# Layer 1's projection as Strassen products of column-tile pairs, with queries and gates kept in DRAM

## The chip, the cores and the metric

One core of one Trainium2 chip runs the whole program. The metric is device microseconds of one execution. Three runs of the kernel before gave 1135.93, 1138.13 and 1138.16 us; the median is 1138.13 us. One further execution was profiled: it took 1137.09 us, of which the trace covers a span of 1135.4 us. TensorE (PE) does the matrix products, VectorE (DVE) and ScalarE (ACT) the element-wise work, GpSimd (POOL) some of it, and SyncE (SP) mostly issues DMAs.

## The reference

A two-layer decoder trunk over 1024 positions of width 1024. Layer 0 is a pooling and short-convolution mixer; layer 1 is sliding-window attention with 16 query heads, 2 key/value heads and a gate. Only layer 1 is changed:

```
y = rms_norm(h, norm_g[1])
proj = y @ w_in + b_in                       # 1024 -> 1024 q | 128 k | 128 v | 1024 z
q = partial_rotary(q.reshape(b, s, 16, 64), cos, sin)     # first 16 dims of each head turn
k = partial_rotary(k.reshape(b, s, 2, 64), cos, sin)
attn = sliding_window_gqa_sinks(q, k, v, sinks)           # 8 blocks of 128 queries, window 128
h = h + (attn * jax.nn.silu(z)) @ w_out + b_out
return rms_norm(h, final_norm_g)
```

## The kernel before

All products are float32-accurate: each operand is split into a high part that TensorE multiplies in its fast float32 mode and a low part that holds the rest (`split`, L179 the cast on ACT, L180 the subtraction on DVE), and three matmuls (high by high, high by low, low by high) stand for one.

**Layer 0's input projection** (to 532 us of the span) is feature-major: the weights are the stationary operand, 512 tokens move. It goes by pairs of column tiles. For each pair, seven products of 4 x 3 matmuls do what eight would do plainly (Strassen's scheme in Winograd's form): three sums of weight quarters before (L409 to L413), seven splits, and five sums of results after (L463 to L477). The products are at L440. Twelve of them are done ahead, with results stored in `c_dram`, while the other operands are still being made.

**Layer 0's output projection** (532 to 718 us, L800 to L802) gives h transposed; each tile gets its residual, is scaled by the norm's gain and split, and is put aside in `h_dram` in another layout (L754, L755).

**Layer 1's projections** are plain: keys and values (`kv`, L186 to L188, 718 to 743 us) and queries (743 to 833 us) are token-major, with h as the stationary operand; each result takes the row's RMS factor and the bias on DVE (L880, L909) and the rotary turn on POOL (L860 to L865). Gates (`gate1`, L1008 to L1018, 833 to about 938 us) are feature-major; DVE multiplies by the RMS row, ACT applies Silu. Queries stay in SBUF as `qt`, gates as `sz`. Block 0's scores run between the gates.

**The attention loop** takes blocks of 128 queries. In its turn `b` it makes the queries' transposed split form for block `b + 1` (`queries`: cast L935, subtraction on POOL L936, transposes on PE L939, copy L941), turns block `b`'s probabilities (`probs`: PE transposes L1058, POOL selects L1064 and L1067), computes scores of `b + 1` (L960, L961; masks and maxima on DVE L963 to L969; Exp on ACT L972), projects block `b - 1` (L1113 to L1115), and attends block `b` (L1081, gate at L1092, split into `aH` and `aL`). `finish` normalises and stores the output (L1129, L1130, L1150). The turn b = 1 begins at 940.2 us, the turn b = 7 at 1098.4, and the last one, which only projects, at 1116.8.

The order on each engine comes from a scheduler that follows dependences; on each engine instructions run strictly in that order, so an instruction that waits holds those behind it. SP issues all DMAs of the kernel before.

Of the kernel before, what the change touches and what calls it, by code (L numbers as in the profile page):

```python
# [78 lines left out]
def trunk(ctx, tc, x, xT, g1, pos, cols, w_in, w_pool, w_out, w_q, w_kv, w_z, b_q, b_kv,  # L79
               sinks, w_o, g_fin, out):  # L80
# [201 lines left out]
    def load_to(n):  # L282
        while len(raws) < min(n, len(units)):
            src, shape, _, _ = units[len(raws)]
            raws.append(W(shape))
            nc.sync.dma_start(out=raws[-1], in_=src)

    def split_to(n):
        load_to(n)
        while len(done) < min(n, len(units)):  # L290
            i = len(done)
            _, shape, alloc, parts = units[i]
            n_ = shape[1] // parts
            res = []
            for j in range(parts):
                h, lo = alloc(F32R), alloc(F32R)
                split(h, lo, raws[i][:, j * n_:(j + 1) * n_])
                res += [(h[:, k, :], lo[:, k, :]) for k in range(n_)]
            done.append(res)
# [945 lines left out]
```

## Time and profile before

| | us |
|---|---|
| median of three runs | 1138.13 |
| profiled execution, whole | 1137.09 |
| its span | 1135.4 |
| PE busy in the span | 1078.5 |
| DVE busy | 783.5 |
| ACT busy | 463.5 |
| POOL busy | 224.6 |

"Busy" counts the time in which an engine has an instruction under way. Matmuls are pipelined, so that one 512-column matmul is listed with about 0.4 us, though another starts every 0.23 us; a stretch where PE is busy all the time is read by the starts. The share over the span hides that stages have different limits, so the rows below are by stage. In rows of groups the columns are: line, engine, operation, output<-input, shapes, count | busy us in all, mean ns of one | idle us of the engine just before, and who ended it.

### The profile page before, as it was taken

Reading aid. Unit: us, or ns where it says so; the run is one execution under the profiler, and the core shown is the slowest. Engines: PE = TensorE matmul, PEld = TensorE weight load, DVE = VectorE, ACT = ScalarE, POOL = GpSimd, SP = SyncE. Lnnn points to the kernel's source line nnn. Section 1 sums busy time; section 2 is a strip of 40 time slices with the busy share of each in tenths; the row PEclk is TensorE's granted clock in tenths of the full one; section 3 lists DMA queues with packets and bytes.
Section 4 is the critical chain, followed back from the end, with each engine's and each line's share of the span. In section 5 each row is a group of like instructions: output and inputs, shape, how many; then the busy total and the mean of one; then the engine's idle time right before and its main releaser. Section 6 shows DMA issues by size and latency. Waiting matters only on the chain.

```text
span 1135.4 us, 14172 instructions
## 1 busy us (share of the span) xinstructions
PE 1078.5 (95%) x5020; PEld 873.1 (77%) x5020; DVE 783.5 (69%) x1392; ACT 463.5 (41%) x961; POOL 224.6 (20%) x396
## 2 busy tenths in 40 slices
PE   4989999999999999999999999999999997898897
PEld 3767788888888888887788788988888885676776
DVE  4699879967696669866645854721143679889995
ACT  4753332423233332334324423320023777777653
POOL 0000000000000000000001010333320226788874
PEclk9999999999999999999999999999999999999999
DMA  5342331221212212126653334410022305370001
GB/s 204 112 167 99 141 128 38 93 84 38 93 38 96 81 56 75 65 75 226 222 203 134 137 142 146 165 38 19 1 93 96 127 24 125 57 93 20 20 20 56
DMA packets 70694, 109.09 MB, mean 96 GB/s; under 512 B 37472, under 2 KB 37600, under 8 KB 70624
## 3 DMA queue, kind: packets, MB, share of 16 engines
q1 hardware_dynamic: 70624, 108.20, 28.9%
q8 instruction: 39, 0.64, 0.2%
q14 instruction: 31, 0.25, 0.1%
HBM read 89.04 MB, written 19.14 MB: 95 GB/s over the span
## 4 chain that ended last, share of the span: by engine, by line
PE 79%; DVE 12%; ACT 5%; issue 2%; DMA 2%; POOL 0%; SPq 0%; DVEq 0%; ACTq 0%
PE b L440 38%; PE psD L801 3%; PE psD L802 3%; PE psA L800 2%; PE psD L800 2%; PE psA L802 2%; PE psA L801 2%; PE psA L186 2%; PE psD L186 2%; PE psA L187 2%; PE psA L188 2%; PE psD L188 2%; PE psD L187 2%; ACT pt L972 1%; DMA W<-w_in 1%
## 5 line engine op out<-in xcount | busy, mean ns | idle before, releaser
L179 ACT CAST W<-W 128x512 fp32r<-128x512 f32 (+1 forms) x199 | 143.9, 731 | 357.9 <-DVE W L180 108.5
L180 DVE TENSOR_TENSOR W<-W 128x512 fp32r<-128x512 f32 (+1 forms) x199 | 162.6, 823 | 115.2 <-ACT W L179 68.6
L690 POOL MEMSET T<- 128x16 f32 x8 | 0.9, 111 | 358.4 <-DVE T L624 229.2
L818 POOL TENSOR_TENSOR t<-t,T 128x512 f32<-128x512 f32 x14 | 19.4, 1387 | 248.5 <-ACT T L817 248.5
L440 PE MATMUL b<-B11h,W 128*128 128x512 f32 x192 | 65.6, 405 | 2.7 <-ACT W L179 1.8
L440 PE MATMUL b<-T2h,W 128*128 128x512 f32 x192 | 64.5, 396 | 2.2 <-ACT W L179 2.2
L440 PE MATMUL b<-B22h,W 128*128 128x512 f32 x192 | 64.7, 398 | 1.2 <-DVE T L469 1.1
L440 PE MATMUL b<-T1h,W 128*128 128x512 f32 x192 | 64.4, 396 | 0.0
L440 PE MATMUL b<-T3h,W 128*128 128x512 f32 x192 | 64.3, 396 | 0.0
L440 PE MATMUL b<-B21h,W 128*128 128x512 f32 x192 | 63.9, 396 | 0.0
L440 PE MATMUL b<-T4h,W 128*128 128x512 f32 x192 | 63.5, 391 | 0.0
L972 ACT ACTIVATE pt<-psB,smax 128x128 f32<-128x128 f32 x128 | 45.4, 366 | 24.8 <-DVE smax L969 19.6
L801 PE MATMUL psD<-U,W 128*128 128x512 f32 x128 | 51.5, 402 | 2.6 <-DVE U L180 2.6
L802 PE MATMUL psA<-U,W 128*128 128x512 f32 x128 | 50.4, 394 | 1.4 <-DVE W L180 1.4
L960 PE MATMUL psB<-kT,qT 128*128 128x256 f32 (+1 forms) x128 | 34.8, 294 | 17.3 <-ACT qT L941 7.6
L802 PE MATMUL psD<-U,W 128*128 128x512 f32 x128 | 50.9, 398 | 0.2 <-DVE W L180 0.2
L800 PE MATMUL psD<-U,W 128*128 128x512 f32 x128 | 51.1, 399 | 0.0
L800 PE MATMUL psA<-U,W 128*128 128x512 f32 x128 | 50.8, 397 | 0.0
L1113 PE MATMUL psD<-O,aH 128*128 128x512 f32 (+1 forms) x128 | 50.7, 396 | 0.0
L801 PE MATMUL psA<-U,W 128*128 128x512 f32 x128 | 50.6, 395 | 0.0
L1115 PE MATMUL psD<-O,aL 128*128 128x512 f32 (+1 forms) x128 | 49.7, 388 | 0.0
L1114 PE MATMUL psD<-O,aH 128*128 128x512 f32 (+1 forms) x128 | 49.6, 387 | 0.0
(330 smaller groups left out, 2923.6 us busy)
## 6 DMA issues: line engine op xcount, KB each, us to landing
W<-w_in SPq DMA_DIRECT2D x54, 512.0 KB, 3.5
W<-w_out SPq DMA_DIRECT2D x32, 512.0 KB, 3.8
W<-w_z SPq DMA_DIRECT2D x16, 512.0 KB, 3.5
O<-o_dram SPq DMA_DIRECT2D x31, 256.0 KB, 5.5
o_dram<-t SPq DMA_DIRECT2D x30, 256.0 KB, 2.0
T<-xT SPq DMA_DIRECT2D x16, 256.0 KB, 4.3
h_dram<-T SPq DMA_DIRECT2D x16, 256.0 KB, 2.1
W<-w_q SPq DMA_DIRECT2D x8, 512.0 KB, 4.4
```

Of the source, the lines that this page charges most:

```text
L179: nc.scalar.copy(out=dst_h, in_=src)
L180: sub(out=dst_l, in0=src, in1=dst_h.bitcast(F32), op=ALU.subtract)
L186: mm(dst, lhsT=ah, rhs=bh, start=(i == 0), stop=False)
L187: mm(dst, lhsT=ah, rhs=bl, start=False, stop=False)
L440: mm(dst, lhsT=w[:, hw, k], rhs=x[hx][:, k], start=start and k + n == 0, stop=k == 3 and n == 2, skip_group_check=not start)
L800: mm(dst, lhsT=w[k][0], rhs=oHL[f][0], start=(f == 0), stop=False)
L801: mm(dst, lhsT=w[k][0], rhs=oHL[f][1], start=False, stop=False)
L802: mm(dst, lhsT=w[k][1], rhs=oHL[f][0], start=False, stop=(f == 15))
L972: exps.append(act(out=res[g][:, 2 * i2 + i, :], in_=bv[:, i, P:256], func=AF.Exp, scale=0.125, bias=smax[:, at + i:at + i + 1], accum_out= ...
L1113: mm(o, lhsT=a[0][:, kk, :], rhs=woH[8 * n + k][:, c], start=(k == 0), stop=False)
L1114: mm(o, lhsT=a[0][:, kk, :], rhs=woL[8 * n + k][:, c], start=False, stop=False)
L1115: mm(o, lhsT=a[1][:, kk, :], rhs=woH[8 * n + k][:, c], start=False, stop=(k == KT - 1))
```

## The change

The class `Strassen` now holds the seven-product scheme, used for layer 0 as before and for layer 1's whole projection (`st1`): nine pairs of column tiles, first the pair (k, v), then four pairs of query tiles, then four of gate tiles. The query columns are reordered so that the first two tiles hold the 16 turning dimensions of all heads.

- `operands` and the norm: h scaled by the gain stays in SBUF as `Y`; the RMS factor is multiplied into it (`normed1`) and the quarters' sums and splits are made (B11, B21, then T1 to T4, B22), partly during layer 0's output projection, partly during 18 products done ahead (`AHEAD1 = 9`), whose results go to `c1_dram` and come back. The RMS sums move from POOL to DVE.
- `kv`: the pair's tiles are transposed on PE to token-major per block. The cos and sin tables are transposed to feature-major.
- `q_pair`, `turn_pair`, `q_store`: bias and turn in feature-major form on DVE, split into high and low, stored to `q_dram`: high from ACT's queue, low from SP's. `load_q` reads them per half block, on POOL's queue; there are no query transposes.
- `z_pair`, `gates`: Silu on ACT, stored to `z_dram` from ACT's queue, read back by SP per half block in `attend`, where one multiplication takes the place of two.
- Scores of blocks 0 and 1, and block 0's probabilities and attention, run between the gate pairs' products; the loop starts at b = 1. Of the eight output weight pieces, four are fetched at the end of the pairs and split as b = 1 begins (`WO_FIRST`), the rest in b = 1 (`WO_PLAN`), all subtractions on DVE.

```
-def queries(b, js): ... for g in range(2):
-            nc.scalar.copy(out=qs[:, :, 0, :], in_=q)
-            ptt(out=qs[:, :, 1, :], in0=q, in1=qs[:, :, 0, :].bitcast(F32), op=ALU.subtract)
-                tr(bank[:, i * P:(i + 1) * P], qs[:, i].rearrange("p a d -> p (a d)"), identr)
-            nc.scalar.copy(out=t, in_=bank.bitcast(F32))
+    def load_q(b, js):
+            for g, t in enumerate(qTs[b, js]):
+                h = 8 * g + 4 * js
+                nc.gpsimd.dma_start(out=t.rearrange("p (h c) -> p h c", c=P), in_=q_dram[
+                    :, :, h:h + 4, b * P:(b + 1) * P].rearrange("a d h c -> (a d) h c"))
+    def queries(b, js):
+        load_q(b, js)
+        load_q(*((b, 1) if js == 0 else (b + 1, 0)))
...
+    st1 = Strassen(w_l1, [(8, 9)] + [(2 * i, 2 * i + 1) for i in (0, 1, 2, 3, 5, 6, 7, 8)],
+                   AHEAD1, c1_dram, ...)
+    st1.store = nc.scalar.dma_start
+    def q_store(t, s, x, biased):
+        hi, lo = t3(F32R), t3()
+        ...
+            act(out=hi, in_=x, func=AF.Identity, bias=col(C_BQ, t))
+            stt(out=lo, in0=x, scalar=col(C_BQ, t), in1=hi.bitcast(F32), op0=ALU.add,
+                op1=ALU.subtract)
+        for j, o in enumerate((hi.bitcast(F32), lo)):
+            (nc.sync if j else nc.scalar).dma_start(out=q_dram[j, 8 * t:8 * t + 8, :, hs(s)]...)
+    def gates():
+        for at_, s_, c in z_out:
+            act(out=c, in_=c, func=AF.Silu, bias=col(C_BZ, at_))
+        for at_, s_, c in z_out:
+            nc.scalar.dma_start(out=z_dram[at_, :, hs(s_)], in_=c)
...
-            tt(out=at[:, 2 * jj:2 * jj + 2, :], in0=at[:, 2 * jj:2 * jj + 2, :],
-               in1=sz[4 * s + 2 * js + jj][:, :, bb * P:(bb + 1) * P], op=ALU.mult)
+        nc.sync.dma_start(out=zt, in_=z_dram[4 * js:4 * js + 4, :, b * P:(b + 1) * P].rearrange(
+            "m p c -> p m c"))
+        tt(out=at, in0=at, in1=zt, op=ALU.mult)
...
-        nc.sync.dma_start(out=out[b * P:(b + 1) * P, :], in_=h2)
+        nc.scalar.dma_start(out=out[b * P:(b + 1) * P, :], in_=h2)
+    for n, k2 in WO_FIRST:
+        load_wo(n, k2)
+    for b in range(1, NB + 1):
```

Three places show how the order moves. ACT's order before, where block 0's Exp (L972) first stands between the gates' Silu (L1018); a table load stands at each change from one function to the other:

```order
L1018 ACTIVATE U<-U,colt 128x512
L179 CAST W<-W 128x1024
L972 ACT_TABLE_LOAD
L972 ACTIVATE pt_7001,den<-psB,smax 128x128 x4
L179 CAST O_7249<-W 128x512
L179 CAST O_7253<-W 128x512
L972 ACTIVATE pt_7002,den<-psB,smax 128x128 x2
L941 CAST qT<-psB 128x512 x2
L972 ACTIVATE pt_7002,den<-psB,smax 128x128 x2
L979 ACTIVATE es<-es 128x8
L1018 ACT_TABLE_LOAD
L1018 ACTIVATE U<-U,colt 128x512
```

ACT's order now, at the same place among the gate pairs (L1117 is Silu, L1092 Exp, L1119 the gates' store):

```order
L1092 ACT_TABLE_LOAD
L1092 ACTIVATE pt_6964,den<-psB,smax 128x128 x2
L180 CAST W<-W 128x512
L1092 ACTIVATE pt_6972,den<-psB,smax 128x128 x2
L180 CAST W<-S_7023 128x512
L1117 ACT_TABLE_LOAD
L1117 ACTIVATE t_6979<-t_6979,colt 128x512
L1092 ACT_TABLE_LOAD
L1092 ACTIVATE pt_6964,den<-psB,smax 128x128 x2
L1092 ACTIVATE pt_6972,den<-psB,smax 128x128 x2
L1092 ACTIVATE pt_6965,den<-psB,smax 128x128 x2
```

The functions change more often: 15 table loads stand from the first of these to block 2's Exp, 7 before from the first shown to the end of the program.

POOL's order before, in one half block of the attention loop (L983 scales the probabilities, L936 is the queries' low part, L1064 and L1067 are selects on the transposed probabilities):

```order
L983 TENSOR_TENSOR pt_8311<-pt_8311,es 128x512
L983 TENSOR_TENSOR pt_8312<-pt_8312,es 128x512
L1064 AFFINE_SELECT pT<-pT 128x512
L936 TENSOR_TENSOR qs<-U,qs 128x4x64 x2
L1067 AFFINE_SELECT pT<-pT 128x512
L1064 AFFINE_SELECT pT<-pT 128x512
L1067 AFFINE_SELECT pT<-pT 128x512
L1064 AFFINE_SELECT pT<-pT 128x512
L1067 AFFINE_SELECT pT<-pT 128x512
L1064 AFFINE_SELECT pT<-pT 128x512
L1067 AFFINE_SELECT pT<-pT 128x512
```

POOL's order now, in one half block (L1103 scales, L1155 and L1158 are the selects, L1053 the queries' loads):

```order
L1103 TENSOR_TENSOR pt_8407<-pt_8407,es 128x512
L1103 TENSOR_TENSOR pt_8408<-pt_8408,es 128x512
L1155 AFFINE_SELECT t_8545<-t_8541 128x512
L1158 AFFINE_SELECT t_8541<-t_8541 128x512
L1155 AFFINE_SELECT t_8546<-t_8542 128x512
L1053 DMA qT<-q_dram 128x4x128
L1158 AFFINE_SELECT t_8542<-t_8542 128x512
L1155 AFFINE_SELECT t_8560<-t_8556 128x512
L1155 AFFINE_SELECT t_8561<-t_8557 128x512
L1158 AFFINE_SELECT t_8556<-t_8556 128x512
L1158 AFFINE_SELECT t_8557<-t_8557 128x512
L1053 DMA qT<-q_dram 128x4x128
```

The two subtractions have gone; two loads stand in their place, one of them in the middle of the selects. A load has to wait until the scores that read its buffer have been computed.

SP's order now, around the start of the loop (W<-h_dram are the eight residual loads, t<-z_dram the gates' reads):

```order
L1176 DMA t_7419<-z_dram 128x4x128
L1032 DMA W<-w_o 128x1024 x4
L1278 DMA W<-h_dram 128x32x32
L1032 DMA W<-w_o 128x1024 x3
L1253 DMA gfin<-g_fin 128x1024
L1032 DMA W<-w_o 128x1024
L1176 DMA t_7578<-z_dram 128x4x128
L1278 DMA W<-h_dram 128x32x32 x4
L1176 DMA t_7770<-z_dram 128x4x128
L1278 DMA W<-h_dram 128x32x32 x3
L1176 DMA t_7909<-z_dram 128x4x128
L1176 DMA t_8065<-z_dram 128x4x128
```

The gates' reads for the half blocks of b = 1 stand behind four and seven of the residual loads.

## Rows read from the trace of the kernel before

**Rows 1.** The page's part 4: the chain that ended last, by engine.

```profile
PE 79%; DVE 12%; ACT 5%; issue 2%; DMA 2%; POOL 0%; SPq 0%; DVEq 0%; ACTq 0%
```

**Rows 2.** Stretches, busy us (count) of PE, PEld, DVE, ACT, POOL; clock, DMA, GB/s.

```profile
50.00:532.00 482.00, 478.56 (x2048) 383.43 (x2046) 377.42 (x626) 163.78 (x272) 1.56 (x14) 1.00 0.26 93
532.00:718.40 186.40, 182.15 (x777) 145.86 (x776) 116.39 (x142) 68.29 (x95) 17.85 (x13) 0.99 0.47 167
718.40:743.00 24.60, 24.60 (x214) 24.57 (x212) 17.30 (x42) 10.10 (x15) 10.08 (x44) 1.00 0.33 119
743.00:833.00 90.00, 90.00 (x404) 73.37 (x403) 19.79 (x28) 7.59 (x12) 30.63 (x96) 1.00 0.05 18
833.00:940.20 107.20, 105.50 (x520) 86.96 (x519) 58.43 (x113) 60.14 (x143) 18.38 (x23) 1.00 0.27 97
940.20:1020.60 80.40, 68.81 (x387) 55.22 (x385) 71.80 (x166) 58.67 (x181) 64.06 (x79) 1.00 0.55 87
1020.60:1098.40 77.80, 68.72 (x385) 55.34 (x383) 71.40 (x173) 53.13 (x174) 60.48 (x76) 1.00 0.07 22
1098.40:1135.40 37.00, 28.90 (x149) 23.11 (x147) 22.41 (x57) 14.22 (x28) 19.50 (x24) 0.95 0.11 43
```

**Rows 3.** Timeline of PE: start, us; forty-eight matmuls lie from the first to the second.

```profile
560.27 0.39 PE L800 MATMUL psD<-U,W 128*128 128x512 f32 x1
...
571.48 0.39 PE L800 MATMUL psA<-U,W 128*128 128x512 f32 x1
```

**Rows 4.** DVE groups in layer 0's projection, 120 to 530 us.

```profile
L180 DVE TENSOR_TENSOR W<-W 128x512 fp32r<-128x512 f32 x120 | 81.9, 687 | 42.8 <-ACT W L179 42.3
...
L673 DVE SCALAR_TENSOR_TENSOR t<-b,colt,t 128x512 f32<-128x512 f32 x16 | 12.0, 751 | 10.5 <-PE b L188 10.5
```

**Rows 5.** ACT's weight casts in the same stretch.

```profile
L179 ACT CAST W<-W 128x512 fp32r<-128x512 f32 x120 | 73.7, 620 | 153.9 <-DVE W L411 61.8 <-PE b L440 53.4 <-PE b L188 16.8
```

**Rows 6.** The small DVE operation after the maxima, from 716 to 945 us.

```profile
L969 DVE SCALAR_TENSOR_TENSOR smax<-smax,nsink 128x2 f32<-128x2 f32 x16 | 2.5, 155 | 0.3
```

**Rows 7.** ACT groups from 833 to 945 us: block 0's and 1's Exp, Silu, table loads.

```profile
L972 ACT ACTIVATE pt<-psB,smax 128x128 f32<-128x128 f32 x32 | 11.4, 370 | 4.0 <-DVE smax L969 2.1 <-PE psB L961 1.8
L1018 ACT ACTIVATE U<-U,colt 128x512 f32<-128x512 f32 x14 | 10.1, 724 | 2.9 <-DVE U L1014 2.8
L972 ACT ACTIVATION_READ_ACCUMULATOR pt<-psB,smax 128x1 f32 x32 | 6.6, 206 | 0.0
...
L1018 ACT ACT_TABLE_LOAD x2 | 2.6, 1283 | 0.0
```

**Rows 8.** DVE groups in one steady block of the loop, 1020.0 to 1046.1 us.

```profile
L966 DVE COPY_PREDICATED psB<-umask,psB 128x256 f32<-128x256 int32 x8 | 3.3, 416 | 0.0
L968 DVE TENSOR_REDUCE smax<-psB 128x2 f32<-128x256 f32 x8 | 3.3, 412 | 0.1
L969 DVE SCALAR_TENSOR_TENSOR smax<-smax,nsink 128x2 f32<-128x2 f32 x8 | 3.1, 392 | 0.1
...
L1092 DVE TENSOR_TENSOR pT<-pT,U 128x256 f32<-128x256 f32 x4 | 2.5, 657 | 0.0
L180 DVE TENSOR_TENSOR aL<-pT,aH 128x512 fp32r<-128x512 f32 x2 | 2.1, 1030 | 0.0
```

**Rows 9.** PE groups in the same block.

```profile
L960 PE MATMUL psB<-kT,qT 128*128 128x256 f32 x16 | 4.5, 306 | 2.8 <-ACT qT L941 1.4 <-DVE smax L969 1.1 <-DVE rs_y L149 0.3
...
L939 PE MATMUL psB<-identr,qs 128*128 128x128 f32 x23 | 2.3, 243 | 0.0
L1058 PE MATMUL psB<-ident,pt 128*128 128x128 f32 x16 | 2.1, 276 | 0.0
```

**Rows 10.** POOL's subtraction for the queries in the same block.

```profile
L936 POOL TENSOR_TENSOR qs<-U,qs 128x256 fp32r<-128x256 f32 x4 | 3.0, 743 | 0.2 <-ACT qs L935 0.2
```

**Rows 11.** SP's issues of the residual loads: count, ns min/median/max; GB/s while three land.

```profile
L1159 SPq DMA_DIRECT2D U<-h_dram x8: 359/377/3562, 952.3 to 1013.1; - x8
GB/s 0 0 0 62 149 199 215 216 218 204 153 146 142 138 150 146 142 137 146 153 148 146 145 146 144 145 137 130 156 156 142 147 147 145 146 144 146 147 145 133
```

More of the change, by code (lines that the diff above doesn't have):

```diff
@@ L34 @@
 W_BUFS = 9
+QT_BUFS = 6
 T3_BUFS = 14
@@ L290, in split_to @@
         while len(done) < min(n, len(units)):
[L291 to L299, printed above, removed]
+            h, lo = W(KP, F32R), W(KP, F32R)
+            split(h, lo, raws[len(done)])
+            done.append([(h[:, k, :], lo[:, k, :]) for k in range(KT)])
     taken = [0]
@@ L480, in trunk @@
-    for n in ("T2", "B11", "T1", "B22", "B21", "T3"):
+    st0 = Strassen(w_in, pairs, AHEAD, c_dram, bank,
+                   lambda i: pools["t3"].tile([P, 4, P], F32, name="S1", bufs=2) if i else
+                   T()[:, 0:HALF].rearrange("p (k c) -> p k c", c=P),
+                   lambda i: t3() if i else T()[:, 0:HALF], True)
+    ops, pair, go_ahead = st0.ops, st0.pair, st0.go_ahead
+    for n in ("T1", "B22", "B21", "T3", "T2", "B11"):
         ops[n] = tuple([bp.tile([P, 4, HALF], F32R, name=f"{n}{'hl'[i]}") for i in range(2)])
@@ new lines, in trunk @@
+    sp_order = contextlib.ExitStack()
+    sp_order.enter_context(tc.manual_schedule(engines={mybir.EngineType.SP}))
+    raw0 = {15: last[0]}
+    for f in range(15):
+        raw0[f] = r0.tile([P, HALF], F32, name="r")
+        nc.sync.dma_start(out=raw0[f], in_=o_dram[f, 0])
+        if f == 7:
+            load_to(2)
+    oHL = operands(0, lambda f: raw0[f])
+    spill(15, 1, last[1])
+    r0.release()
+    p0.release()
+    yp = tc.alloc_tile_pool(name="y1", bufs=1, reuse_waits="tile")
+    Y = {n: yp.tile([P, 4, HALF], F32, name=f"y{n}") for n in ("11", "21", "12", "22")}
@@ new lines, in trunk, with kv @@
+    khl = {}
+    def kv(b):
+        s, bb = divmod(b, 4)
+        bank = psB()
+        for j in range(2):
+            tr(bank[:, j * P:(j + 1) * P], kvt[j, s][:, bb * P:(bb + 1) * P], ident)
+        kk = p1_.tile([P, 2, 1, HD], F32, name="kk")
+        tt(out=kk.rearrange("p a b d -> p (a b d)"), in0=bank[:, 0:P], in1=bkv[:, 0:P], op=ALU.add)
+        tt(out=vtok[:, b, :], in0=bank[:, P:256], in1=bkv[:, P:256], op=ALU.add)
+        rotary(kk[:, :, 0, :], 2, b)
+        kh = p1_.tile([P, 2, 2, HD], F32R, name="kh", bufs=3)
+        kl = p1_.tile([P, 2, 2, HD], F32R, name="kl", bufs=3)
+        kd = kk.to_broadcast([P, 2, 2, HD])
+        nc.scalar.copy(out=kh, in_=kd)
+        tt(out=kl, in0=kd, in1=kh.bitcast(F32), op=ALU.subtract)
+        khl[b] = (kh, kl)
@@ new lines, in q_pair, with done @@
+    def q_pair(i):
+        o = {n: t3() for n in ((0, 1), (1, 0), (1, 1))}
+        def done(s):
+            if i:
+                for j in range(2):
+                    q_store(2 * i + j, s, o[j, s], False)
+            else:
+                kv_steps.insert(2 + 4 * s, lambda: turn_pair(s, o[0, s], o[1, s]))
+        steps = between()
+        steps[3].append(lambda: done(0))
+        st1.pair(1 + i, [o[0, 1], o[1, 0], o[1, 1]], lambda c: o.setdefault((0, 0), c), steps,
+                 lambda: done(1))
@@ L1155, in trunk @@
             steps = []
-            if prev is not None and js == (1 if b == 1 else 0):
-                h2 = big.tile([P, D], F32, name="U")
+            if js == 0:
+                h2 = W([P, D])
                 sb, bb = divmod(b - 1, 4)
```

878 lines of the change are left out of this document (450 added, 428 removed).

## The prediction

> **What bounds the kernel now.** I read the chain of waits first: 79% of the span hangs on PE, 12% on DVE [rows 1]. That is a mean over stages, so next the stretches [rows 2]. The reader is to see two kinds. Up to 940.2 us PE never rests for long: 478.6 busy of 482 in layer 0's projection, 90.0 of 90.0 in the query stage, 105.5 of 107.2 among the gates, while DVE has 19.8 of 90 and 58.4 of 107. There PE alone sets the time, and DVE has room to take work. From 940.2 to 1098.4 it is otherwise: six turns of the loop in 158.2 us (26.4 each), PE busy 137.5 of them, DVE 71.8 of 80.4 and 71.4 of 77.8 (89 and 92%), ACT and POOL at 68 to 80%. PE's waits there are for DVE and ACT in turn [rows 9]. The clock is 1.00, except at the very end. So PE work taken away before 940 us is worth its full time only as long as DVE, which takes over work, stays beside PE; in the loop what counts is DVE.
>
> **The change part by part.** First PE's work of the new projection. Another 512-column matmul starts every (571.48 - 560.27) / 48 = 0.2335 us [rows 3]. Before, keys and values cost 24.6 us and queries 90.0 [rows 2]; in matmuls, 192 of half width for keys and values and 768 of full width for queries and gates, the worth of 864. Now there are nine pairs of seven products of twelve, 756. The difference, 108 x 0.2335, is 25.2 us, and nothing else in the change takes as much away. Against it stand 32 float32 transposes (keys, values, tables) at 2.1 us for 16 [rows 9], 4.2 us. PE's own schedule from 718.4 us on:
> - 18 products ahead: 216 x 0.2335 = 50.4 us.
> - 45 products: 540 x 0.2335 = 126.1; transposes above 4.2; 32 transposes of keys at 0.1 (L939: 2.3 for 23, [rows 9]) 3.2; scores of block 0 and 1, 16 + 32 half-width matmuls at 0.117, 5.6; block 0's probabilities and attention 16 transposes and 8 matmuls, 4.0. Together 143.1.
>
> If PE alone decided, turn b = 1 would begin at 718.4 + 50.4 + 143.1 = 911.9 instead of 940.2.
>
> **DVE beside it.** For the 45 products: 45 subtractions of splits, 36 weight sums and 45 combinations, 126 x 0.687 = 86.6 us [rows 4]; keys and values 24 small operations, at most 0.416 each (L966, [rows 8]), 10.0; the turn 8 x 0.751 + 4 x 0.687 = 8.8 [rows 4]; the queries' low parts, 12 at 0.751 and 4 at 0.687, 11.8; scores of two blocks, 16 x (0.416 + 0.412 + 0.155) [rows 6, 8] and sink terms, 17.4; block 0's probabilities and attention 8.3. Sum 143, against PE's 143. The plain stages had DVE at 22 to 54%; layer 0's pairs had 377.4 of 482, 78%, with PE at 99% [rows 2]. Here DVE stands at 100% of PE's time, and the nearest row for an engine in that position is DVE in the loop, 92%. 143 / 0.92 = 155 us.
>
> ACT adds its own bound among the gate pairs. Their work on it: 20 casts x 0.620 [rows 5] = 12.4; 16 Silu x 0.724 = 11.6; Exp of 32 heads 11.4 + 6.6 = 18.0; 15 table loads x 1.283 = 19.2 [rows 7]; 16 stores issued at some 0.38 (SP's issue, [rows 11]) = 6; copies and splits 7. Sum 74 us against PE's 66 (20 products 56.0, scores and block 0's attention). This, too, gives about 155: the key and query pairs at PE's 77, the gate pairs at 74 / 0.95 = 78. The Trainium skill (ScalarE: Activation LUTs, "What ACT_TABLE_LOAD costs") adds a drain of 1.38 us to each change of the table; by that 15 loads would cost 40 us instead of 19, the gate pairs would end 21 us later, and the time would be 1144. The rows give the load 1.283, no idle time before the Silu pair (0.0), and 2.8 of the 2.9 us before Silu itself to DVE [rows 7], so the sum keeps 1.283, and the rule gets no more than a small part of the second rival's chance.
>
> The 18 products ahead: DVE has 18 splits, and in pieces of 512 columns 8 of the norm, 16 of the quarters' sums and 20 of low parts, 62 x 0.687 = 42.6 us [rows 4], beside PE's 50.4. I add 1 us for the first products' wait on the second half's RMS factor (51.5). Turn b = 1 then begins at 718.4 + 51.5 + 155 = 925, 15.3 us earlier. The RMS sums that go to DVE in layer 0's output projection, 15 x 0.687 = 10.3 us and the first quarters' norm and splits, are hidden by the room there: DVE 116.4 of 186.4 [rows 2]; without it they would cost those 10 us.
>
> **The loop.** Per turn DVE loses two of four gate multiplications, 1.3 us (L1092, 2.5 for 4) less some 0.3 for their greater width; PE 16 query transposes at 0.1, ACT four casts and four copies, POOL 3.0 us of subtractions [rows 10]. POOL matters for DVE: the small operation after the maxima takes 155 ns before the loop and 392 in it, the low part of the attention 1030 instead of 687 [rows 6, 8]. POOL's 3.0 us less of some 20 should give DVE 0.5 back. 71.4 / 3 - 1.5 = 22.3 us of DVE at 92% is 24.2 us a turn; I take 25.1 with what the new loads cost, the middle between that and the steady stretch's 25.9 [rows 2].
>
> The loads' cost has no row. POOL issues four query loads a turn: from below nothing, as SP needs 0.38 us [rows 11], less than the 0.743 of the subtraction that goes [rows 10]; from above a POOL instruction of 0.743 each, and the wait of the selects behind a load whose buffer is still being read: up to 2.5 us per half block, the length of PE's scores of it (16 x 0.117 + waits of 1.4, [rows 9]). I take 0.4 per half block. SBUF — State Buffer, "SBUF: two separate sides" in the Trainium skill, says that a load issued by POOL is starved while DVE holds the port that they share, 0.62 us becoming 3.1; if each of the 24 loads of the loop came 2.5 us late on the path, that would be 60 us, a time of 1183, the far end of the third rival. The trace has no load on POOL's queue; only the stretched DVE rows show the shared port.
>
> Once, as the loop begins: eight subtractions of output weights (twice 0.687 each, 11 us on DVE), where before three pieces remained for the loop, partly on POOL: +6. The gates' reads for b = 1 stand on SP behind four and seven residual loads; three of those land in some 10 us, 145 GB/s [rows 11], so the reads come up to 13 us after the issue of the first. If the loads start during the last gate pair, as their buffers permit, most is over when the reads are needed; below 0, above 13, I take 2. What is late next is DVE, whose gate multiplication waits with maxima behind it. Six turns: 6 x 25.1 + 8 = 159, as before (158.2).
>
> The last two stretches, 37.0 us [rows 2], have no queries to make; the output store on ACT's queue and the wider gate multiplication give 36.5.
>
> **Sum.** 925 + 159 + 36.5 = 1120.5 of span; 1.7 us lie around it (1137.1 - 1135.4); the median of the runs is 1.0 above the profiled execution: 1123 us, 15 less than 1138.1 (1.3%).
>
> **Rivals.**
> - PE remains the bound to the end of the pairs. For it: 99% with DVE at 78% [rows 2], and the splits of a later product are made three products ahead. Against: DVE and ACT have no slack in sum. Then b = 1 at 912, turns of 24.2 and 4 us at the start: 912 + 149 + 36.5 + 2.7 = 1100 us.
> - The gain is eaten within the pairs. Five combinations a pair must follow the bank of the product, each with splits and maxima queued before and behind; Silu, Exp and table loads alternate on ACT. If DVE reaches only 84% of a 143 us load, as far below the loop's 92 as this is below full, the pairs take 170 us: 1138, no change.
> - The loop gets slower, by one mechanism: POOL's queries wait at the head of its queue for PE's scores to free a buffer, the selects behind it wait, PE's projection and attention wait for the selects. Price: the wait beyond 0.4 us per half block, twelve of them; the gain is gone at 1.7 us, and at 2.5, the upper bound, 12 x 2.1 = 25 us: 1148, slower than before. For it: the load stands between two selects of the same half block, and POOL is busy 78% of the loop [rows 2]. Against: six buffers, of which a half block uses two.
>
> That the change doesn't do what it says can be excluded: the queries' transposes and subtractions are gone from the order.
>
> **Chances.** Forecast 0.52, full saving 0.16, gain eaten 0.14, slower loop 0.18. The forecast's own range is 1110 to 1133 (pairs 147 to 163 us, start of the loop 0 to 13). The whole range, leaving out a part of the slow loop and the best of the full saving, is 1097 to 1150. A measurement of this kernel tells apart some 0.2% (2.3 us). Faster: 0.16 + nearly all of 0.52 + a fifth of 0.14 = 0.68; same 0.09; slower 0.18 + what is left, 0.23.
>
> **What would show it.** In the profile after: layer 0 as long as before; the 18 products ahead at 0.2335 us per matmul, some 51 us; the pairs at 155 us with DVE over 90% busy and PE waits ended by DVE's combinations in the query pairs and by ACT's Silu and Exp in the gate pairs; first transpose of turn 1 near 925; turns of about 25 us. Wrong are: pairs at PE's pace (full saving) or over 163; a POOL that waits for PE's scores with selects behind; the first turns longer than 33 us because of the gates' reads; or a query or gate load that lands after its user is ready in every turn.

## The result and the profile after

Four runs of the changed kernel took 1149.99 to 1155.97 us, median 1153.01; the kernel before took 1137.03 beside them. The ratio is 1.0141 (95% interval 1.0109 to 1.0173): 1.4% slower, where 15 us less were forecast, and above the range. The profiled execution is the fastest of the four, with a span of 1148.3 us.

The forecast was a sum of four stretches, so the first reading is the same cut [rows 2]: from the start of the span to the last product made ahead, the first and second half of the pairs, turn 1, turn 2, turns 3 to 6, the end. A turn starts with PE's first transpose of block `b`'s probabilities. Windows of the kernel after (columns as in rows 2):

```profile
0.00:768.70 768.70, 742.35 (x3204) 597.46 (x3205) 559.25 (x874) 304.35 (x481) 12.27 (x44) 0.99 0.35 121
768.70:850.70 82.00, 76.57 (x366) 62.06 (x364) 63.28 (x114) 32.68 (x62) 13.92 (x48) 1.00 0.48 166
850.70:933.20 82.50, 72.51 (x328) 59.19 (x329) 58.56 (x127) 54.42 (x122) 17.70 (x20) 0.92 0.83 226
933.20:971.50 38.30, 26.00 (x113) 19.53 (x111) 28.71 (x43) 20.30 (x43) 20.25 (x24) 0.87 1.40 181
971.50:1000.60 29.10, 23.21 (x112) 18.39 (x113) 25.65 (x57) 15.54 (x52) 21.44 (x27) 0.94 0.45 85
1000.60:1106.50 105.90, 91.79 (x450) 71.69 (x449) 94.93 (x225) 58.42 (x202) 77.72 (x99) 0.95 0.27 68
1106.50:1148.30 41.80, 31.86 (x153) 25.30 (x151) 23.30 (x61) 16.48 (x41) 20.93 (x25) 0.86 0.14 51
```

| stretch, us | forecast | after | difference |
|---|---|---|---|
| products ahead end at | 769.9 | 768.7 | -1.2 |
| the 45 products of the pairs | 155 | 164.5 | +9.5 |
| six turns | 159 | 173.3 | +14.3 |
| end | 36.5 | 41.8 | +5.3 |
| span | 1120.5 | 1148.3 | +27.8 |

(The stretches are rounded, hence the last tenth.) The saving on PE came: turn 1 begins at 933.2 instead of 940.2. Then turn 1 takes 38.3 us, turns 2 to 6 take 27.0 each, where before it was 29.3 and 25.7, and the end 41.8 instead of 37.5. (By PE's first transpose turn 7 of the kernel before begins at 1097.9, not at 1098.4, so its end is 37.5 here.) The loop gives back more than the projection gained.

**The steady turns.** Groups of the kernel after from 1000.61 to 1082.18 us (line, engine, operation, shapes, count; busy us, mean ns; idle before), of DVE:

```profile
L1089 DVE SCALAR_TENSOR_TENSOR smax<-smax,nsink 128x2 f32<-128x2 f32 x25 | 19.5, 778 | 0.0
...
L181 DVE TENSOR_TENSOR aL<-t,aH 128x512 fp32r<-128x512 f32 x6 | 6.9, 1151 | 0.0
L1182 DVE TENSOR_TENSOR t<-t,t 128x512 f32<-128x512 f32 x6 | 5.3, 881 | 0.0
```

and of POOL:

```profile
L1158 POOL TENSOR_SCALAR_AFFINE_SELECT t<-t 128x512 fp32r<-128x512 f32 x24 | 18.7, 785 | 1.3 <-DVE t L181 0.8
L1155 POOL TENSOR_SCALAR_AFFINE_SELECT t<-t 128x512 fp32r<-128x512 f32 x24 | 15.4, 648 | 0.0
...
L1053 POOL DMA_DIRECT2D qT<-q_dram x10 | 7.9, 790 | 0.0
```

The small operation after the maxima, on two numbers per partition, takes 778 ns; it was 392 in the loop before [rows 8] and 155 ahead of it [rows 6]. A query load costs POOL 0.790 us, two per half block 1.6, where the prediction took 0.4. Its idle time of 0.0 says that in these turns it did not wait for PE: POOL is simply busy with issuing it. POOL's time in a turn is therefore much what it was, as the windows of turns 2 to 6 show (before, then after; POOL is the fifth engine):

```profile
969.50:1097.85 128.35, 113.13 (x634) 91.85 (x634) 115.20 (x280) 90.44 (x288) 101.31 (x128) 1.00 0.28 46
971.52:1106.48 134.96, 114.98 (x560) 90.06 (x561) 120.55 (x281) 73.94 (x254) 99.14 (x125) 0.95 0.31 71
```

That is 20.3 us of POOL a turn before and 19.8 after, in turns of 25.7 and 27.0: the relief of POOL on which the sum counted did not come, and POOL's time in sum is not what lengthened the turns. One place shows how a two-number operation becomes PE's wait. The timeline of POOL in the kernel after (start, us, engine, line, operation):

```profile
1024.43 1.22 POOL L1155 TENSOR_SCALAR_AFFINE_SELECT t<-t 128x512 fp32r<-128x512 f32 x2
1025.61 1.22 POOL L1158 TENSOR_SCALAR_AFFINE_SELECT t<-t 128x512 fp32r<-128x512 f32 x2
1026.79 0.77 POOL L1053 DMA_DIRECT2D qT<-q_dram  x1
1027.57 1.28 POOL L1269 TENSOR_TENSOR W<-W,gfin 128x512 f32<-128x512 f32 x1
```

beside that of DVE,

```profile
1025.60 3.27 DVE L1089 SCALAR_TENSOR_TENSOR smax<-smax,nsink 128x2 f32<-128x2 f32 x1
1028.80 0.75 DVE L1086 COPY_PREDICATED psB<-umask,psB 128x256 f32<-128x256 int32 x2
```

of ACT (in brackets idle time, and what ended it),

```profile
1028.97 0.37 ACT L1092 ACTIVATE pt<-psB,smax 128x128 f32<-128x128 f32 x1 [2.37 <-DVE smax L1089]
```

and of PE:

```profile
1029.83 0.66 PE L1149 MATMUL psB<-ident,pt 128*128 128x128 f32 x4 [2.01 <-ACT pt L1092]
```

DVE's operation begins at 1025.60 and ends at 1028.87, with POOL's unbroken row (1027.57 + 1.28 = 1028.85). The load stands in that row and lengthens it. Exp waits for the operation, and PE's transposes for Exp. (This is one place; no run shows how much of a turn goes this way.) The Trainium skill (SBUF — State Buffer, "SBUF: two separate sides") says that a DVE operation with two SBUF inputs and a POOL operation that reads SBUF lock the shared port from each other, and that the loser blocks fully. This trace agrees that DVE blocks, and through several POOL instructions in a row. The load itself is not starved as the prediction had weighed from that page: 0.79 us each, not 3.1.

**The start of the loop.** Timeline of SP's queue in the kernel after:

```profile
940.84 0.38 SPq L1176 DMA_DIRECT2D t<-z_dram  x1
941.31 11.44 SPq L1278 DMA_DIRECT2D W<-h_dram  x4
952.79 3.55 SPq L1176 DMA_DIRECT2D t<-z_dram  x1
```

The gates that block 0's second half needs were stored by ACT at 934.4 and 935.5, just before. The read waits for the store to land (SP's waits between 925 and 960 us; what waits, for what: us, times, longest),

```profile
SPq L1176 <- DMA z_dram<-t: 7.5, 2, 4.8
```

and DVE waits for the read, with the weight subtraction and PE behind it:

```profile
944.26 0.69 DVE L1182 TENSOR_TENSOR t<-t,t 128x512 f32<-128x512 f32 x1 [5.25 <-DMA t<-z_dram]
944.87 1.22 DVE L181 TENSOR_TENSOR U<-W,U 128x1024 fp32r<-128x1024 f32 x1
```

```profile
947.28 0.80 PE L1203 MATMUL psD<-U,aH 128*128 128x512 f32 x1 [6.14 <-DVE U L181]
```

**The pairs.** PE's waits there, all of them, from 768.7 to 933 us (what waits, for what: us, times, longest):

```profile
PE psB L1149 <- issue: 3.5, 1, 3.5
PE b L387 <- DVE t L441: 2.9, 1, 2.9
PE b L387 <- DVE W L181: 2.7, 1, 2.7
PE b L387 <- DVE t L432: 2.6, 1, 2.6
PE psB L1149 <- DVE t L1181: 2.4, 1, 2.4
PE psB L1149 <- POOL pt L1103: 1.2, 1, 1.2
PE psB L1080 <- ACT pt L1092: 0.2, 1, 0.2
```

They sum to 15.5 us; PE's own 143.1, as forecast, and these make 158.6. Of the other 6, a part can be read as slower matmuls: after the wait for L181,

```profile
874.50 4.63 PE L387 MATMUL b<-U,W 128*128 128x512 f32 x10 [2.67 <-DVE W L181]
878.93 0.31 PE L1080 MATMUL psB<-kT,qT 128*128 128x128 f32 x1
```

ten matmuls take 4.43 us, 0.443 each instead of 0.2335 [rows 3], which is 2.1 us too much, and the window has a granted clock of 0.92. DVE's busy time in the pairs is 63.3 + 58.6 = 121.8 us, not 143.

### The profile page after: what moved, and what is told of

Its sections match the earlier page's. It is cut to its first block, busy times and chain, and to the rows that moved or that the text cites. A ratio compares the mean times of both kernels' runs of the same rounds, so it can differ in the third digit from the quotient of the medians.

```text
span 1148.3 us, 13822 instructions
## 1 busy us (share of the span) xinstructions
PE 1064.3 (93%) x4720; PEld 853.6 (74%) x4720; DVE 853.7 (74%) x1495; ACT 502.2 (44%) x1000; POOL 184.2 (16%) x285
## 5 line engine op out<-in xcount | busy, mean ns | idle before, releaser
L181 DVE TENSOR_TENSOR W<-W 128x512 fp32r<-128x512 f32 (+1 forms) x234 | 177.6, 768 | 106.7 <-ACT W L180 65.9
L387 PE MATMUL b<-U,W 128*128 128x512 f32 x432 | 109.8, 407 | 5.2 <-DVE W L181 2.7
L387 PEld LDWEIGHTS b<-U,W 128*128 128x128 f32 x432 | 81.8, 194 | 23.5 <-DVE W L181 3.1
L387 PE MATMUL b<-B22h,W 128*128 128x512 f32 x264 | 88.4, 396 | 3.0 <-DVE t L441 3.0
L387 PE MATMUL b<-B11h,W 128*128 128x512 f32 x264 | 88.7, 401 | 2.1 <-ACT W L180 1.2
L387 PE MATMUL b<-B21h,W 128*128 128x512 f32 x264 | 87.5, 396 | 1.1 <-ACT W L399 1.1
L387 PE MATMUL b<-T2h,W 128*128 128x512 f32 x192 | 65.4, 402 | 2.4 <-ACT W L180 2.4
L1092 ACT ACTIVATE pt<-psB,smax 128x128 f32<-128x128 f32 x128 | 45.7, 365 | 48.2 <-DVE smax L1089 32.3
L387 PE MATMUL b<-T1h,W 128*128 128x512 f32 x192 | 64.4, 396 | 0.0
L387 PE MATMUL b<-T3h,W 128*128 128x512 f32 x192 | 64.2, 395 | 0.0
L387 PE MATMUL b<-T4h,W 128*128 128x512 f32 x192 | 63.2, 390 | 0.0
L387 PEld LDWEIGHTS b<-B11h,W 128*128 128x128 f32 x264 | 50.4, 191 | 15.0 <-ACT W L180 1.6
L387 PEld LDWEIGHTS b<-B22h,W 128*128 128x128 f32 x264 | 49.6, 188 | 15.6 <-ACT t L985 3.3
L387 PEld LDWEIGHTS b<-B21h,W 128*128 128x128 f32 x264 | 49.6, 188 | 13.7 <-ACT W L399 2.0
L1203 PE MATMUL psD<-U,aH 128*128 128x512 f32 (+1 forms) x128 | 52.1, 407 | 6.9 <-DVE U L181 6.9
L1202 PE MATMUL psD<-U,aH 128*128 128x512 f32 (+1 forms) x128 | 53.6, 419 | 2.2 <-ACT U L180 2.2
L827 PE MATMUL psD<-U,W 128*128 128x512 f32 x128 | 51.3, 401 | 2.6 <-DVE U L181 2.6
L387 PE MATMUL b<-B11l,W 128*128 128x512 f32 x132 | 52.9, 401 | 0.8 <-DVE B11l L471 0.8
L387 PE MATMUL b<-B21l,W 128*128 128x512 f32 x132 | 52.1, 395 | 0.0
L387 PE MATMUL b<-B22l,W 128*128 128x512 f32 x132 | 52.0, 394 | 0.0
```

Of the source, the lines that this page charges most:

```text
L181: sub(out=dst_l, in0=src, in1=dst_h.bitcast(F32), op=ALU.subtract)
L387: mm(dst, lhsT=w[:, hw, k], rhs=x[hx][:, k], start=start and k + n == 0, stop=k == 3 and n == 2, skip_group_check=not start)
L827: mm(dst, lhsT=w[k][0], rhs=oHL[f][1], start=False, stop=False)
L1092: act(out=res[g][:, 2 * i2 + i, :], in_=bv[:, i, P:256], func=AF.Exp, scale=0.125, bias=smax[:, at + i:at + i + 1], accum_out=den[:, at + ...
L1202: mm(o, lhsT=a[0][:, kk, :], rhs=woH[8 * n + k][:, c], start=(k == 0), stop=False)
L1203: mm(o, lhsT=a[0][:, kk, :], rhs=woL[8 * n + k][:, c], start=False, stop=False)
```

## The experiments

Each was timed in three rounds beside the kernel before, which had a median of 1136.7 (E1 to E4), 1137.05 (E5 to E8) and 1136.84 (E9 to E11). Stretches are from each one's profiled execution.

| kernel | median us | ratio [95%] | turn 1 begins | turn 1 | turns 2 to 6, each | end |
|---|---|---|---|---|---|---|
| before | 1137.03 | | 940.2 | 29.3 | 25.7 | 37.5 |
| after | 1153.01 | 1.0141 [1.0109, 1.0173] | 933.2 | 38.3 | 27.0 | 41.8 |
| E1 maxima in PSUM | 1141.85 | 1.0039 [1.0021, 1.0058] | 932.9 | 34.9 | 26.7 | 41.4 |
| E2 last gates kept | 1144.89 | 1.0067 [1.0043, 1.0090] | 938.1 | 30.5 | 26.9 | 40.1 |
| E3 queries by SP | 1127.88 | 0.9921 [0.9894, 0.9948] | 929.6 | 35.7 | 23.5 | 40.9 |
| E4 no table changes | 1143.51 | 1.0054 [1.0033, 1.0075] | 937.3 | 30.9 | 26.2 | 41.2 |
| E5 POOL busy instead | 1134.75 | 0.9985 [0.9975, 0.9996] | 933.5 | 37.1 | 24.4 | 39.9 |
| E6 E3 and E2 | 1121.80 | 0.9878 [0.9854, 0.9901] | 932.6 | 30.3 | 23.5 | 40.6 |
| E7 E1, E2 and E3 | 1120.60 | 0.9865 [0.9847, 0.9883] | 929.5 | 28.6 | 24.0 | 40.9 |
| E8 before, maxima in PSUM | 1131.45 | 0.9958 [0.9946, 0.9971] | 939.0 | 27.4 | 25.2 | 37.0 |
| E9 plain loads by POOL | 1152.17 | 1.0132 [1.0102, 1.0162] | 935.9 | 38.3 | 26.9 | 40.3 |
| E10 tiny loads by POOL | 1146.93 | 1.0078 [1.0051, 1.0106] | 936.0 | 36.8 | 26.2 | 41.4 |
| E11 half by POOL | 1148.48 | 1.0105 [1.0072, 1.0138] | 931.3 | 37.4 | 26.3 | 42.2 |

Two things have to be known for reading this table. First, the loads are not spread evenly. Of the 32 query loads the kernel after issues 14 before turn 1, four in each of turns 1 to 4, two in turn 5 and none in turn 6; in every version with the change turns 3 to 5 hold about ten of the loads and turn 6 none. Secondly, an edit changes more than its lines: the scheduler orders DVE, ACT and POOL anew for each version (PE's order is the same in all). By the traces, over turns 3 to 5:

| version | order of DVE, ACT and POOL, loads aside | turns 3 to 5, each | turn 6 |
|---|---|---|---|
| after, E9 | one order, the same instruction for instruction | 27.2, 27.2 | 24.3, 25.3 |
| E2, E11 | the same, but for a few instructions of DVE and ACT | 27.3, 26.3 | 25.2, 25.2 |
| E4, E10 | a second, shared by both | 28.0, 27.5 | 23.4, 23.5 |
| E1 | the second on POOL, nearly so on ACT, another on DVE | 27.5 | 23.8 |
| E3, E6 | a third, the same but for a few instructions of DVE | 23.5, 23.5 | 23.6, 23.5 |
| E5, E7 | POOL's and DVE's differ from the third | 25.1, 23.7 | 23.5, 23.7 |

So with both loads of a half block issued by POOL turns 3 to 5 take 27.2 to 28.0 us, in two different orders, and with neither, and nothing in their place, 23.5 to 23.7, again in more than one order. In turn 6, without loads, all versions lie between 23.4 and 25.3. If turn 6 stands for a turn without loads, the loads cost 2 to 3 us a turn in the first order (E9, after) and 4 to 4.5 in the second (E10, E4), and the order alone is worth up to 1.9.

**E1.** Is it DVE's small operation alone? The maxima go to two dead columns of the scores' PSUM bank, so that only one input of the operation lies in SBUF.

```diff
-            nc.vector.tensor_reduce(out=m, in_=bv[:, :, P:256], axis=AX.X, op=ALU.max)
-            stt(out=m, in0=m, scalar=-0.125, in1=nsink[:, 8 * js + at:8 * js + at + 2],
+            mx = bv[:, 0, 0:2]
+            nc.vector.tensor_reduce(out=mx, in_=bv[:, :, P:256], axis=AX.X, op=ALU.max)
+            stt(out=m, in0=mx, scalar=-0.125, in1=nsink[:, 8 * js + at:8 * js + at + 2],
```

> The changed kernel, but the maxima of the scores go to a dead column of their PSUM bank, so that the small operation after them (L1089) reads one input from PSUM and one from SBUF, not two from SBUF. Theory A (this operation waits for POOL's back-to-back selects: 778 ns instead of 155, 3 times 3.6 us too much in three turns): it falls to under 0.2 us, the steady turns from 27.2 to 25 us or less, the clock in them comes back towards 1.00, the whole 12 to 18 us less, 1135 to 1141. Theory B (the loop is set by the lowered clock and by PE's own chain, DVE's stretched operation lies beside it): the operation gets short as well, but turns stay at 26.5 to 27.5 and the time within 3 us of 1153.

It is 11 us faster, but turns 2 to 6 stay at 26.7. DVE's groups of this kernel, 985 to 1082 us:

```profile
L1099 DVE TENSOR_TENSOR es<-sink,smax 128x8 f32<-128x8 f32 x7 | 5.2, 737 | 0.1
L1090 DVE SCALAR_TENSOR_TENSOR smax<-psB,nsink 128x2 f32<-128x2 f32 x28 | 4.0, 151 | 0.1
```

The operation no longer waits (151 ns), but the next one with two SBUF inputs now does (737 ns). In the kernel after the same operation took 167 in that window:

```profile
L1098 DVE TENSOR_TENSOR es<-sink,smax 128x8 f32<-128x8 f32 x7 | 1.2, 167 | 0.2
```

POOL's own waits in E1's window, two of them:

```profile
POOL pt L1104 <- DVE es L1102: 14.5, 6, 4.6
POOL qT L1053 <- PE psB L1081: 4.5, 2, 2.3
```

So here the load does stand at the head of POOL's queue until PE's scores free the buffer, as the third rival had it. That goes with the order as much as with DVE: E4 and E10, with the same order on POOL, show the same wait (1.4 and 3.5 us in this window) without the edit. They also give the fairer comparison for it. In E4 the small operation takes

```profile
L1089 DVE SCALAR_TENSOR_TENSOR smax<-smax,nsink 128x2 f32<-128x2 f32 x28 | 13.7, 489 | 0.1
```

and turns 3 to 5 take 28.0 us, in E1 151 ns and 27.5. The stretched operation is a carrier of the delay, not its cause: remove it, and the turn is nearly as long by another way.

**E2.** Is it the gates' read at the start? Block 0's second half takes the last pair's two gates from SBUF.

```diff
-        tt(out=at, in0=at, in1=zt, op=ALU.mult)
+        tt(out=at[:, 0:n], in0=at[:, 0:n], in1=zt[:, 0:n], op=ALU.mult)
+        for jj in range(n, 4):
+            tt(out=at[:, jj], in0=at[:, jj], in1=z_keep[jj - 2, 0][:, 0:P], op=ALU.mult)
```

> The changed kernel, but block 0's second half takes the gates of the last pair from SBUF instead of from DRAM; all else goes through DRAM as before. Theory A (the last pair's round trip Silu, store, load is exposed at the start of turn 1: DVE waits 5.2 us for it, PE 6.1): the wait goes, PE's longest wait in turn 1 under 2 us, 5 to 7 us less, 1146 to 1148. Theory B (the output weights' pieces, fetched and split there, are as late): PE waits 4 us or more for their splits and the time falls by under 2 us.

Turn 1 falls from 38.3 to 30.5, though in the profiled execution it also began 4.9 later; its end is 3 us earlier, the median 8 us lower. The wait for the gates has gone, but PE still waits 3.0 us once in turn 1, for ACT's cast of an output weight, where theory A had under 2. The round trip is real and is the smaller part.

**E3.** Is it POOL issuing the loads? The tile is declared float32 and read as float32r, so that SP can issue them.

```diff
-            qTs[b, js] = [pe.tile([P, HALF], F32R, name="qT", bufs=QT_BUFS) for _ in range(2)]
+            qTs[b, js] = [pe.tile([P, HALF], F32, name="qT", bufs=QT_BUFS) for _ in range(2)]
...
-                nc.gpsimd.dma_start(out=t.rearrange("p (h c) -> p h c", c=P), in_=q_dram[
+                nc.sync.dma_start(out=t.rearrange("p (h c) -> p h c", c=P), in_=q_dram[
...
-        return qTs.pop((b, js))
+        return [t.bitcast(F32R) for t in qTs.pop((b, js))]
```

> The changed kernel, but SP issues the queries' loads (as plain float32 loads), POOL none. Theory A (the loads' issue on POOL, 0.79 us each, lengthens the unbroken row of selects that DVE waits behind): L1089 falls from 778 to some 600 ns, a turn by 0.5 to 1 us, 3 to 6 us less. Theory B (POOL's loads lie in time that POOL has): within 2 us; Theory C (on SP they queue behind the residual loads and the gates' reads): slower by 3 us or more, with PE waiting for queries in turns 1 and 2.

25 us faster than the kernel after, and faster than before; theory A had the direction, at 3 to 6 us. Turns 2 to 6 take 23.5 us. Windows (the pairs, turn 1, turns 2 to 6, the end):

```profile
768.70:929.56 160.86, 147.65 (x690) 120.30 (x689) 120.45 (x240) 86.72 (x184) 22.00 (x54) 0.97 0.61 199
929.56:965.30 35.74, 26.22 (x113) 19.66 (x112) 27.36 (x50) 21.86 (x49) 17.87 (x21) 0.86 1.29 197
965.30:1082.80 117.50, 108.57 (x562) 85.04 (x561) 108.54 (x275) 73.10 (x251) 89.89 (x111) 1.00 0.30 83
1082.80:1123.60 40.80, 30.74 (x153) 24.67 (x151) 22.79 (x59) 15.87 (x37) 20.60 (x25) 0.90 0.14 52
```

PE and DVE are each busy 92% of the steady turns, at full clock. DVE's small operation in them is back to what it took before the change:

```profile
L1089 DVE SCALAR_TENSOR_TENSOR smax<-smax,nsink 128x2 f32<-128x2 f32 x34 | 13.6, 401 | 0.1
```

The six turns take 153.2 us here and 173.3 after: 20.1 less, or 1.7 for each of their twelve half blocks, the prediction's unit (only nine hold loads). This is the price of the loads on POOL together with the order that comes with them. Turns 2 to 5, which hold loads, differ by 4.2 us each, turn 6 by 0.7.

**E4.** Do the table loads bound the pairs? Tanh stands in for Silu, which leaves out the right gate, and all but two of the table loads go.

```diff
-            act(out=c, in_=c, func=AF.Silu, bias=col(C_BZ, at_))
+            act(out=c, in_=c, func=AF.Tanh, bias=col(C_BZ, at_))
```

> The changed kernel with Tanh in place of Silu for the gates (this leaves the right gate out), which has its table together with Exp, so that 14 of the table loads among the gate pairs go, 18 us of ACT. Theory A (ACT bounds the gate pairs): the pairs end 8 to 14 us earlier, turn 1 begins at 920 to 925 instead of 933, the time falls by as much. Theory B (DVE and the reads back from DRAM set the pairs' pace): turn 1 begins at 930 or later, under 3 us gained.

Turn 1 does not begin earlier (937.3): the table loads are not the bound of the pairs, whatever a load costs beyond its 1.283 us. The time still falls by 9.5 us, against both theories. What is faster lies at the start of the loop and in turn 2 (23.6 us against 29.1), under another order; why was not followed up.

**E5.** Is it POOL's time alone? SP loads as in E3, and for each load POOL writes two selects into its buffer first.

```diff
+                for i in range(2):
+                    nc.gpsimd.affine_select(out=t[:, 256 * i:256 * i + 256].bitcast(F32R), in_=jk, pattern=[[1, 256]],
+                                            compare_op=ALU.is_ge, fill=0.0, base=0,
+                                            channel_multiplier=-1)
+                nc.sync.dma_start(out=t.rearrange("p (h c) -> p h c", c=P), in_=q_dram[
```

> The changed kernel with the queries loaded by SP, and on POOL, where each load's issue stood, two selects of 128x256 into the load's buffer before it (together about 0.7 us). Theory A (what the loads on POOL cost is POOL's time and place between the selects of the attention, not the way of their transfer): turns return from 23.5 to 26.5 to 27.5 us and the time from 1128 to 1143 to 1155. Theory B (a transfer issued by POOL is itself the harm, by its descriptors or its late landing): turns stay at 23.5 to 24.5, the time at 1126 to 1134.

The selects took, from 985 to 1082 us,

```profile
L1056 POOL TENSOR_SCALAR_AFFINE_SELECT qT<-jk 128x256 fp32r<-128x256 f32 x24 | 11.3, 472 | 0.3 <-PE psB L1087 0.3
```

0.94 us per load, more than the load's issue. POOL is busy as long as in the kernel after, 20.1 us a turn (turns 2 to 6):

```profile
970.51:1092.34 121.83, 108.65 (x562) 86.86 (x561) 110.65 (x272) 71.68 (x245) 100.60 (x139) 0.99 0.29 81
```

and yet turns 2 to 6 grew by 0.9 only, of the 3.5 us between E3 and after (turns 3 to 5 by 1.6 of 3.7). That is theory B's range for the turns and just above it for the time: POOL's time alone is a quarter to under a half of the price. E5's order is not E3's, so these shares are rough.

**E6, E7.** Do the cures add up? E6 has the edits of E3 and E2, E7 those of E1 as well, as shown above; in E7 the maxima's line is

```diff
+            stt(out=m, in0=mx, scalar=-0.125, in1=nsink[:, 8 * js + at:8 * js + at + 2],
```

and in both the two lines that matter most are

```diff
+                nc.sync.dma_start(out=t.rearrange("p (h c) -> p h c", c=P), in_=q_dram[
...
+        n = 2 if (b, js) == (0, 1) else 4
```

> Queries loaded by SP, and block 0's second half takes the last pair's gates from SBUF. Theory A (the two losses are separate): 5 to 8 us less than with SP's queries alone, 1120 to 1123, PE's wait of 6 us in turn 1 gone. Theory B (SP's queries have already taken the wait's place in turn 1, where now residual loads, gates and queries stand on one queue): within 2 us of 1128.

> As before, and the maxima of the scores in PSUM. Theory A (in turns of 23.5 us DVE is the bound at over 90%, and its small operation after the maxima is still 388 instead of 155 ns, 1.9 us a turn): turns of 22 to 22.8, 5 to 10 us less than without it, 1112 to 1117. Theory B (POOL's selects and PE's chain set these turns): turns of 23 to 23.5, within 3 us of the run without it.

Loads by SP and kept gates: 31 us less than after. The maxima in PSUM add nothing that can be told from none (the intervals overlap; turns 2 to 6 take 24.0 us, in another order of DVE). E7 has the lowest median, 1.35% below the kernel before. Its pairs:

```profile
768.70:929.53 160.83, 147.41 (x692) 119.72 (x691) 122.09 (x241) 84.94 (x183) 21.25 (x54) 0.98 0.60 200
```

**E8.** The edit of E1 in the kernel before, on its own lines L968 and L969.

```diff
+            mx = bv[:, 0, 0:2]
```

> The kernel before with the maxima of the scores in PSUM; nothing else. Theory A (its turns of 25.9 are bound by DVE, 92%): the small operation falls from 364 to some 155 ns, 1.7 us a turn, turns of 24.3 to 25, 5 to 10 us less than 1137. Theory B (the chain over ACT, POOL and PE sets them): turns of 25.5 to 26, within 3 us of 1137.

0.4% or 5.6 us faster, within theory A's 5 to 10, but by other ways than its turns: half a microsecond a turn in turns 2 to 6, and 1.8 in turn 1. Here, too, the wait went on to the next operation (L979, 662 ns; L978 before, 317, both from 985 to 1082 us), and DVE's order changed. The stretched operation cost little before, too.

**E9.** Is it the change of type on the way? POOL issues the loads, into float32 tiles.

```diff
-            qTs[b, js] = [pe.tile([P, HALF], F32R, name="qT", bufs=QT_BUFS) for _ in range(2)]
+            qTs[b, js] = [pe.tile([P, HALF], F32, name="qT", bufs=QT_BUFS) for _ in range(2)]
```

> The changed kernel, all query loads issued by POOL as in it, but as plain float32 transfers without the change of type to TensorE's float32 mode: a control, since SP's loads differed from the changed kernel's in that too. Theory A (the issue by POOL is the harm): turns of 26.5 to 27.5 and 1148 to 1156, as the changed kernel. Theory B (the change of type in the transfer is): turns near 23.5, 1126 to 1132.

As slow as the kernel after. The Trainium skill (DMA: Bandwidth & Descriptors, "SWDGE vs HWDGE vs iDMA") counts a load into float32r as a cast, which only POOL can issue; here the cast costs nothing, for the order and turns 3 to 5 (27.2 us) are those of the kernel after. Its window from 985 to 1082 us also clears the clock:

```profile
985.00:1082.00 97.00, 79.73 (x404) 61.63 (x405) 87.57 (x195) 51.19 (x174) 73.20 (x95) 1.00 0.23 77
```

a granted clock of 1.00, where the kernel after has 0.93 in the same window, and turns as long. The lower clock of the kernel after does not make its turns long.

**E10.** Is it the bytes? SP loads, after a load of a sixteenth of the bytes in as many pieces, issued by POOL into the same buffer.

```diff
+                nc.gpsimd.dma_start(out=t.rearrange("p (h c) -> p h c", c=P)[:, :, 0:8], in_=q_dram[
+                    :, :, h:h + 4, b * P:b * P + 8].rearrange("a d h c -> (a d) h c"))
+                nc.sync.dma_start(out=t.rearrange("p (h c) -> p h c", c=P), in_=q_dram[
```

> Queries loaded by SP, and before each of these loads POOL issues one of a sixteenth of the bytes (8 of 128 columns) with as many pieces into the same buffer. Theory A (what POOL does to issue a transfer, its time and the port it holds, decides): L1053 takes about 0.79 us again, turns of 26 to 27.5, 1145 to 1153. Theory B (the bytes by POOL's queue, their landing, decide beyond the 0.8 us): turns near those of the selects put in their place, 24.7, and 1131 to 1137.

```profile
L1053 POOL DMA_DIRECT2D qT<-q_dram x13 | 10.1, 780 | 3.5 <-PE psB L1083 3.5
```

The issue takes 0.780 us for 16 KB, 0.790 for 256 KB. The comparison that holds the order is with E4, where POOL issues the whole loads: 27.5 us here against 28.0 in turns 3 to 5. So it is not the bytes that POOL's queue moves. Against E3 turns 2 to 6 are 2.7 us longer, three times what E5's selects cost, but two more things differ there: the order, and that SP's loads now wait until POOL's have landed (SP's waits from 970 to 1082 us):

```profile
SPq L1055 <- DMA qT<-q_dram: 84.3, 15, 9.2
```

**E11.** Is it in proportion? One of each two loads by POOL, the other by SP.

```diff
-                nc.gpsimd.dma_start(out=t.rearrange("p (h c) -> p h c", c=P), in_=q_dram[
+                (nc.sync if g else nc.gpsimd).dma_start(out=t.rearrange("p (h c) -> p h c", c=P), in_=q_dram[
```

> POOL issues the loads of the first key group's queries, SP those of the second: half the dose, plain transfers. Theory A (each load on POOL costs alike): half of the 25 us, 1138 to 1143, turns of 25 to 25.7. Theory B (the second load of a half block, behind the first, is what lengthens the row of selects): 1128 to 1133, turns under 24.5.

Neither theory's number. Against E3 half of the loads seem to cost 2.8 of the 3.5 us a turn, but E11 has the order of the kernel after, not E3's. Within that order its turn 6, without loads, takes 25.2 us; turns 3 to 5 take 26.3 with one load a half block on POOL, and 27.2 with two (after, E9). At a kept order, then, the second load of a half block adds about what the first does, some 1 us a turn, if turn 6 stands for a turn without loads.

## Why the prediction was wrong

**The failed step** is the loads' term in the loop: "I take 0.4 per half block", and with it POOL's 3.0 us of relief. The issue measured 0.79 us per load, 1.6 per half block, so POOL got 3.2 us in a turn with four loads in place of the 3.0 that went, where the sum let it have 3.0 less. By E3 against after the loads on POOL, with the order that comes with them, cost the loop 20 us, 1.7 per half block. The bounds were right (0 to 2.5), the value taken lay near the wrong row: SP's issue of 0.38, not the POOL instruction of 0.743 [rows 10] that the load resembles, and whose place it takes. The count was wrong, too: 18 loads lie in the loop, not 24. That an edit has the scheduler set the loop in another order had no term in the sum; turn 6, without loads, puts it at 0.7 us (after) to 1.7 (E9) a turn. The third rival named the place and, at 1.7 us, the point at which the gain is gone; but its waiting for PE's scores is 0.5 us in the kernel after from 985 to 1082 us, and 1.4 to 4.5 in E1, E4 and E10. In the kernel after, the load delays by being issued, in an unbroken row of POOL's work behind which, at the place read above, DVE's operation with two SBUF inputs stands.

**The start of the loop** (+8 for it): the residual loads ahead of the gates' reads were seen, not that the first read waits for a store of the gate pair just made. Kept gates give back 6.1 us in the median with loads by SP (E6 against E3), 8.1 without. Turn 1 of E6 is 6.8 us over a steady turn, near the 8 allowed.

**The pairs** (155, measured 164.5; 161 in E3 and E7): above the 163 that the prediction called wrong, and wrong in cause. DVE's load of 143 came from means of 0.687; back to back such operations start 0.61 apart (944.26 and 944.87 in DVE's rows at the start of the loop), each beginning before the one ahead has ended. In the pairs the durations of DVE's 240 operations add up to 136.6 us and cover 121.8. DVE is busy 74% of the pairs, and taking away ACT's table loads did not shorten them (E4). PE pays 15.5 us for seven single waits, of which those before L387 (8.2) are for a combination or a split, and some 6 besides, in part at the lower clock behind them. DVE itself waited there for results read back from `c_dram`, which the sum did not hold:

```profile
DVE t L432 <- DMA t<-c_dram: 9.3, 2, 8.3
```

Which of these to remove was not tried.

**The products ahead** came out to 1.2 us, so PE's saving was sized rightly.

**The sum** fits E6, which lacks the two faults: its median is 1121.8 against 1123. That is partly luck: its turn 1 begins 7.6 us late, its six turns take 147.6 instead of 159, and its end 40.6 instead of 36.5. DVE is busy 92% of its steady turns, as forecast, but with 21.7 us of work instead of 22.3; that this is POOL's relief is not shown, for in E3, with the same order, the small operation is no shorter than before (401 against 392).

**Open:** what in an issue by POOL costs more than the same time in selects, which no run compares at a kept order; what makes one order of the loop dearer than another; what adds 2 to 5 us to the end in every version with the change; and why E1 and E4 gain 11 and 9.5 us in the median while turns 3 to 5 stay.
